# Layer 0: the prompt's value products two blocks later in the output projection

## The chip, the cores and the metric

The kernel runs on one core of one Trainium2 chip. The metric is the device time of one execution in microseconds (us). The time before the change is the median of three runs, and one execution was also taken by the hardware profiler. Engines are named as in the profile: PE (matrix multiply) with PEld (its weight loads), DVE (vector), ACT (scalar), POOL, and SP, which issues most of the transfers.

## The reference

The reference is one inference step of a two-layer decoder, for a prompt of 256 tokens and a group of 8 single-token samples that share all weights (264 columns together). Layer 0 does a root-mean-square norm, one input projection to q, k, v, bu and bv, block-sparse attention with 8 heads of 64 (on the prompt this is plain causal softmax attention in two 128-row blocks, since the block is 256 long), a gated mixer on bu and bv, and one output projection, then a feed-forward network with a causal convolution of width 3. Layer 1 has stick-breaking attention and a pooling mixer in place of the two mixers. The part of layer 0 that matters here:

```
p = softmax(q k^T / 8, causal)            # prompt, per head
a = p v                                   # "value products"
y = concat(a, b_out) @ w_out              # output projection
x = x + y
```

The samples attend to 256 cached keys and values each, plus their own.

## The kernel before

**Tiles.** Activations lie transposed: 128 features on the partitions and 264 columns (256 prompt, 8 samples) along the free side. A weight block is 128x128. Weights and operands are 32-bit; each is cut into a high and a low part (`wh`/`wl`, `catA_h`/`catA_l`), and each weight block takes three matmuls: high weight by high operand, high weight by low operand, low weight by high operand. All weight blocks of the kernel stand in one hand-written order, 1472 of them, in phases `in0`, `out0`, `ff0`, `dn0`, `in1`, and so on. `in0` has 160 blocks, so block 169 of the kernel is block 9 of `out0`.

**Weights.** `raw(ci)` loads a chunk of 8 or 16 blocks from memory (tile `raw`), issued by SP; `split(t)` cuts 8 blocks at a time, the high part on ACT and the low part on DVE (line 324).

**The order of out0.** `run(order, rhs, evac, hooks)` walks the blocks and issues their matmuls (line 228 is the one line through which all matmuls go, 231 all transposes). The output projection has 8 result tiles (m) of 8 blocks (k). For the first four m the blocks k = 4..7, which read `catB` (the gated mixer), come first: 16 blocks. Then the same four m take k = 0..3, which read `catA` (attention): 16 blocks. Then come the other four m. So the first block that reads `catA` is block 16 of `out0` (block 176 of the kernel), with `catA[:, 0]`; blocks 17, 18 and 19 read `catA[:, 1]`, `[:, 2]` and `[:, 3]`.

**Hooks.** `blk(b, f)` calls `f` once `b` blocks of the phase have been issued; that is how other work on PE is put between weight blocks. In `in0` to `out1` every PE instruction is pinned to the order in which the program issues it (`fixed[0] = True`). On ACT and DVE only some instructions are pinned (`keep_in_program_order`) or tied behind one named instruction (`behind`); the rest is put in order when the program is built, by a planner that goes by its own estimates of when inputs are ready, and among ready instructions takes the one that was issued first. On the chip each engine then runs its own list.

**The work around the change.** At hook 1 of `out0`, 20 of the samples' value reductions are issued (`sm_value`, line 606, DVE, pinned). At hook 4 come `sm_out` (transposes `po_l`, copies `part_l`, additions into `osam_l`), `v_turn` (transposes `vtp_v` of v, copies to `vt` on ACT, line 638) and `sm_cut` (high part of the samples' result on ACT, line 515; low part on DVE, line 519). At the hook of the change, `s_av(t)` is called for four pairs of heads: 4 matmuls of `pT` (softmax weights, transposed) and `vt` into the PSUM tile `pav0_t`, and then `halves`, which copies the high part (`catA_h<-pav`, ACT, line 515) and the low part (`catA_l<-pav,catA_h`, DVE, line 519). In the profile a 32-bit matmul of that kind appears twice, so the four calls of a layer are 32 rows. For t > 0 the low part is tied behind the samples' low part:

```
halves(catA[0][:, t, :SEQ], catA[1][:, t, :SEQ], pav[:, :SEQ])
if t > 0:
    behind(held_by[0], st0["cut"])
```

At hook 15 `hold(23)` and `hold(24)` tie the cuts of weight tiles 23 and 24: the DVE half behind the last low part of `s_av`, the ACT half of tile 24 behind the samples' high part. Layer 1 calls its own value products, `z_av`, at hook 11 of `out1`.

Of the kernel before, what the change touches and what calls it, by code (L numbers as in the profile page):

```python
# [215 lines left out]
def tile_decoder_step(ctx: ExitStack, tc: tile.TileContext, a):  # L216
# [828 lines left out]
    blk = lambda b, f, *x: hk.at(b / 8 - 1, f, *x)  # L1045
# [66 lines left out]
    blk(15, hold, 23)  # L1112
    blk(15, hold, 24)
    for t in range(4):
        blk(9, s_av, t)
    blk(24, lnexp)


# [189 lines left out]
    blk = lambda b, f, *x: hk.at(b / 8 - 1, f, *x)  # L1308
# [163 lines left out]
```

## Time and profile before

| | before |
|---|---|
| median of 3 runs | 587.07 us (586.77 to 587.13) |
| profiled execution | 587.01 us |
| its span | 585.1 us |
| granted PE clock | 0.998 |
| PE busy | 578.1 us, 99% |
| PEld busy | 567.1 us, 97% |
| DVE busy | 444.9 us, 76% |
| ACT busy | 342.1 us, 58% |
| POOL busy | 47.7 us, 8% |
| moved by the transfers | 128.81 MB, mean 220 GB/s |

The span is what the profile covers; the profiled execution took 1.9 us more than its span. Times in the views below count from the start of the span. A row of the timeline gives the start, the duration, the engine, the line, the operation, the tile written and the tiles read, and in brackets the idle time of the engine before it and what ended it. Matmuls overlap: each lasts about 0.28 us in the record, while a new one starts every 0.12 us, so the distance of starts is what counts.

### The profile page before, as it was taken

The page shows a single profiled execution, that of the slowest core. Times are in us where ns is not written, and L with a number is a line of the kernel's source. Part 1 is how long each engine was busy: PE and PEld are TensorE (multiplying, and loading weights), DVE is VectorE, ACT ScalarE, POOL GpSimd, SP SyncE. Part 2 cuts the span into 40 slices and gives each one's busy share as a digit, 9 for nine tenths or more (in the row PEclk, how much of TensorE's full clock was granted, in tenths as well). Part 3 has the DMA queues.
Part 4 walks back from the last instruction along what each step waited for, and adds up shares of the span by engine and source line. Part 5 has one row for each costly group of instructions (what it writes and reads, how often), then busy time and mean ns, then how long its engine had stood idle before and what let it go on. Part 6 is the DMA issues. An engine that isn't in the chain of part 4 may idle for free.

```text
span 585.1 us, 12476 instructions
## 1 busy us (share of the span) xinstructions
PE 578.1 (99%) x4928; PEld 567.1 (97%) x4928; DVE 444.9 (76%) x867; ACT 342.1 (58%) x612; POOL 47.7 (8%) x62
## 2 busy tenths in 40 slices
PE   9999999999999999999999999999999999999995
PEld 8998989999999999999999889999999999999995
DVE  6999898887777778656658879977787787865561
ACT  7848848755555656544445467667565565664431
POOL 1000205300000000001130000120000000011011
PEclk9999999999999999999999999999999999999999
DMA  8999798545454555985467779655454545454502
GB/s 328 409 371 397 228 320 308 203 159 196 165 189 171 184 178 165 346 311 194 162 249 253 289 220 286 216 205 192 170 201 160 211 156 211 155 213 153 207 1 75
DMA packets 29964, 128.81 MB, mean 220 GB/s; under 512 B 3826, under 2 KB 5842, under 8 KB 18514
## 3 DMA queue, kind: packets, MB, share of 16 engines
q1 hardware_dynamic: 29472, 127.50, 61.9%
q8 instruction: 39, 0.64, 0.4%
q10 hardware_dynamic: 434, 0.51, 0.3%
q14 instruction: 19, 0.16, 0.1%
HBM read 123.94 MB, written 4.06 MB: 219 GB/s over the span
## 4 chain that ended last, share of the span: by engine, by line
PE 97%; issue 1%; POOL 0%; POOLq 0%; DVE 0%; ACT 0%; ACTq 0%
PE mm L228 91%; PE sc L228 1%; PE pav L228 1%; PE warm L228 1%; PE pt L231 1%; PE Z L228 1%; PE S L228 1%; PE pv_l L228 0%; PE pf L228 0%; PE pm L228 0%; PE vtp_v L231 0%; POOL yo L1398 0%; PE po_l L231 0%; PE vtp_sgu L231 0%; POOLq L1447 0%
## 5 line engine op out<-in xcount | busy, mean ns | idle before, releaser
L324 ACT ACTIVATE wh<-raw 128x1024 fp32r<-128x1024 f32 x177 | 187.4, 1060 | 194.8 <-PE mm L228 182.1
L324 DVE TENSOR_TENSOR wl<-raw,wh 128x1024 fp32r<-128x1024 f32 x177 | 217.3, 1229 | 100.7 <-ACT wh L324 99.9
L228 PE MATMUL mm<-xg_f_h,wh 128*128 128x264 f32 x704 | 200.8, 285 | 0.0
L228 PE MATMUL mm<-xg_f_h,wl 128*128 128x264 f32 x704 | 200.7, 285 | 0.0
L228 PE MATMUL mm<-xg_f_l,wh 128*128 128x264 f32 x704 | 199.6, 283 | 0.0
L228 PEld LDWEIGHTS mm<-xg_f_l,wh 128*128 128x128 f32 x704 | 133.1, 189 | 0.0
L228 PEld LDWEIGHTS mm<-xg_f_h,wh 128*128 128x128 f32 x704 | 132.8, 189 | 0.0
L228 PEld LDWEIGHTS mm<-xg_f_h,wl 128*128 128x128 f32 x704 | 132.5, 188 | 0.0
L228 PE MATMUL mm<-a_h,wh 128*128 128x264 f32 x352 | 100.4, 285 | 0.0
L228 PE MATMUL mm<-a_h,wl 128*128 128x264 f32 x352 | 100.4, 285 | 0.0
L228 PE MATMUL mm<-a_l,wh 128*128 128x264 f32 x352 | 99.8, 283 | 0.0
L228 PEld LDWEIGHTS mm<-a_l,wh 128*128 128x128 f32 x352 | 66.6, 189 | 0.0
L228 PEld LDWEIGHTS mm<-a_h,wh 128*128 128x128 f32 x352 | 66.4, 189 | 0.0
L228 PEld LDWEIGHTS mm<-a_h,wl 128*128 128x128 f32 x352 | 66.3, 188 | 0.0
L228 PE MATMUL mm<-xg_h,wh 128*128 128x264 f32 x160 | 42.8, 293 | 0.0
L228 PE MATMUL mm<-xg_h,wl 128*128 128x264 f32 x160 | 41.7, 284 | 0.0
L228 PE MATMUL mm<-xg_l,wh 128*128 128x264 f32 x160 | 41.5, 284 | 0.0
L228 PE MATMUL mm<-xg_n_h,wh 128*128 128x264 f32 x128 | 37.0, 289 | 0.0
L228 PE MATMUL mm<-xg_n_h,wl 128*128 128x264 f32 x128 | 36.6, 286 | 0.0
L228 PE MATMUL mm<-xg_n_l,wh 128*128 128x264 f32 x128 | 36.4, 285 | 0.0
L228 PEld LDWEIGHTS mm<-xg_h,wh 128*128 128x128 f32 x160 | 28.9, 191 | 1.6 <-issue 1.2
L228 PEld LDWEIGHTS mm<-xg_h,wl 128*128 128x128 f32 x160 | 28.7, 189 | 0.0
(268 smaller groups left out, 864.7 us busy)
## 6 DMA issues: line engine op xcount, KB each, us to landing
raw<-in_w SPq DMA_DIRECT2D x89, 1024.0 KB, 4.8
K<-in_kt SPq DMA_DIRECT2D x32, 256.0 KB, 5.2
V<-in_vt SPq DMA_DIRECT2D x24, 256.0 KB, 6.3
pb_l<-zd_l SPq DMA_DIRECT2D x24, 256.0 KB, 5.3
V<-in_vp SPq DMA_DIRECT2D x8, 256.0 KB, 7.6
raw<-in_w SPq DMA_DIRECT2D x3, 512.0 KB
xw<-in_xw SPq DMA_DIRECT2D x3, 388.0 KB
X<-in_x SPq DMA_DIRECT2D x2, 528.0 KB
```

The source lines that it names most:

```text
L228: return self.keep(nc.tensor.matmul(*x, **k))
L231: return self.keep(nc.tensor.transpose(*x, **k))
L324: for i, j in zip((s.activation(h, src, AF.Copy), v.tensor_tensor(l, src, h.bitcast(F32), ALU.subtract)), ahead.pop(tt, ())):
```

## The change

The four calls of `s_av` are hooked at block 11 of `out0` instead of block 9: on PE, the six matmuls of blocks 169 and 170 of the kernel (`catB` by the weights of the third result tile) now stand ahead of the value products instead of behind them. Nothing is added or removed, and no other hook stands between 9 and 11.

```diff
     blk(15, hold, 23)
     blk(15, hold, 24)
     for t in range(4):
-        blk(9, s_av, t)
+        blk(11, s_av, t)
     blk(24, lnexp)
```

## The prediction

> **What bounds the kernel now.** I read the page's head and the chain that ended last first, to see which engine sets the time; then the chain in order of time, for the place of the change; then the timelines of PE, ACT and DVE there, for the waits that the move could add or remove.
>
> ```profile
> span 585.1 us, 12476 instructions
> PE 578.1 (99%) x4928; PEld 567.1 (97%) x4928; DVE 444.9 (76%) x867; ACT 342.1 (58%) x612; POOL 47.7 (8%) x62
> PE 97%; issue 1%; POOL 0%; POOLq 0%; DVE 0%; ACT 0%; ACTq 0%
> PE warm L228 <- PEq L1438: 0.8, 1, 0.8
> ```
>
> The last line is all that the view of waits has for PE: one wait, before the first instruction. Everything else is a stream of matmuls. So the time changes only if the number or the pace of PE's instructions changes, or if PE starts to wait. A move that lets PE find its inputs sooner has nothing to take away. In all, 585.1 - 578.1 = 7.0 us of the span are without PE, and they lie outside the place of the change: the 0.8 us at the start, and what follows the last matmul.
>
> In the chain in order of time (start, us, what) the value products of both layers stand so:
>
> ```profile
> 81.83 2.80 PE pav L228 x32
> ...
> 364.20 2.80 PE pav L228 x32
> ```
>
> The 32 rows take 2.80 us in layer 0 at block 9 of its phase, and 2.80 us in layer 1, where they already stand at block 11 of a phase in the same order (`catB` first, then `catA`). That is the nearest row to the changed place, and it says that the place costs PE nothing by itself.
>
> **The change part by part.** PE's timeline around the place (start, us, engine, line, operation, tiles):
>
> ```profile
> 81.55 0.28 PE L228 MATMUL mm<-catB_h,wl 128*128 128x264 f32 x1
> 81.76 2.87 PE L228 MATMUL pav<-pT,vt 128*64 128x256 f32 x32
> 84.57 0.39 PE L228 MATMUL mm<-catB_h,wh 128*128 128x264 f32 x1
> 84.79 0.28 PE L228 MATMUL mm<-catB_l,wh 128*128 128x264 f32 x1
> ...
> 85.41 0.29 PE L228 MATMUL mm<-catB_h,wh 128*128 128x264 f32 x1
> ...
> 86.14 0.29 PE L228 MATMUL mm<-catB_h,wh 128*128 128x264 f32 x1
> ...
> 87.23 0.29 PE L228 MATMUL mm<-catA_h,wh 128*128 128x264 f32 x1
> 87.36 0.28 PE L228 MATMUL mm<-catA_l,wh 128*128 128x264 f32 x1
> ...
> 88.34 0.29 PE L228 MATMUL mm<-catA_h,wh 128*128 128x264 f32 x1
> 88.47 0.28 PE L228 MATMUL mm<-catA_l,wh 128*128 128x264 f32 x1
> ```
>
> *Six matmuls pass in front.* From 85.41 to 86.14 six matmuls start in 0.73 us. That is how much later the value products come: start 82.49 instead of 81.76, end of their stretch 85.30 instead of 84.57. Behind them 15 matmuls are left until `catA` instead of 21. The same work stands between 81.55 and 87.23, so `catA` is asked for at 87.23 as before. The price is 0.
>
> *Going into and out of the value products.* From the last full matmul to the first product is 81.76 - 81.55 = 0.21 us against 0.12 at pace, and from the first matmul behind them to the second 84.79 - 84.57 = 0.22: some 0.09 and 0.10 us of changeover. Both are there once before and once after, between blocks of the same result tile either way (blocks 8 to 11 are one tile). Price 0; if the place mattered, the bound from these two rows is plus or minus 0.2 us. I take 0, since layer 1 shows the same 2.80 us at block 11.
>
> *What the products wait for.* They read `vt`, whose copies are on ACT:
>
> ```profile
> 80.08 1.09 ACT L638 ACTIVATE vt<-vtp_v 128x512 f32<-128x512 f32 x2
> 82.70 0.38 ACT L515 ACTIVATE catA_h<-pav 128x256 fp32r<-128x256 f32 x1 [1.53 <-PE pav L228]
> ...
> 84.67 0.38 ACT L515 ACTIVATE catA_h<-pav 128x256 fp32r<-128x256 f32 x1 [0.27 <-PE pav L228]
> 86.55 0.23 ACT L515 ACTIVATE catA_h<-osam_l 128x32 fp32r<-128x32 f32 x1 [1.49 <-DVE osam_l L955]
> 89.03 2.01 ACT L324 ACTIVATE wh<-raw 128x1024 fp32r<-128x1024 f32 x2 [2.26 <-DMA raw<-in_w]
> ```
>
> `vt` is done at 81.17, 0.59 us before the products start, so nothing waited for it. The move makes this slack 1.32 us. That gains nothing, because the 0.59 was already above zero.
>
> *The high parts, on ACT.* Four copies follow the products, from 82.70 to 85.05. They move by 0.73: 83.43 to 85.78. ACT then sat idle until 86.55, waiting for the samples' result on DVE, and after that until 89.03 for a weight transfer. The delay fits into the first gap with 86.55 - 85.78 = 0.77 us to spare. Price 0.
>
> *The low parts, on DVE*, are what PE's `catA` blocks need last:
>
> ```profile
> 79.11 0.41 DVE L606 CUSTOM_DVE_ANT_1 pb_l<-pb_l,V 128x256 f32<-128x256 f32 x1
> ...
> 86.03 0.18 DVE L949 TENSOR_TENSOR ob<-ob,v 128x32 f32<-128x32 f32 x1
> ...
> 86.43 0.42 DVE L519 TENSOR_TENSOR catA_l<-pav,catA_h 128x256 fp32r<-128x256 f32 x1
> 86.81 0.19 DVE L519 TENSOR_TENSOR catA_l<-osam_l,catA_h 128x32 fp32r<-128x32 f32 x1
> 86.92 1.08 DVE L519 TENSOR_TENSOR catA_l<-pav,catA_h 128x256 fp32r<-128x256 f32 x3
> 87.91 1.21 DVE L324 TENSOR_TENSOR wl<-raw,wh 128x1024 fp32r<-128x1024 f32 x1
> ```
>
> From 79.11 to 86.03 DVE goes through the 20 value reductions of the samples without a gap, and these do not depend on the products. The first low part could have run at 83.08, when its high part was done, and ran at 86.43. After the move its input is there at 83.81: still 2.62 us of cover. The fourth has its input at 85.78 and starts at about 87.6. So DVE's times stay, and with them the end of the last low part, 86.92 + 1.08 = 88.00, which PE reads at 88.47. The margin of 0.47 us that PE has there is set by DVE, not by the products, and is untouched. If DVE had been free, the price would still be zero until the high parts came later than about 87.2. The cut of the next weight tile (87.91) stands behind the last low part and stays too; so do the transfers, which are issued as buffers come free behind such cuts.
>
> *PSUM banks.* The four `pav` tiles are freed by the low parts, whose times stay; nothing that follows them sooner is asked for.
>
> Sum: 0 on PE, 0 through ACT, 0 through DVE. Against the profiled execution's own 587.01 us (span 585.1 and 1.9 around it) that is 587.0 us; the median of the three runs is 587.07, 0.01% away. 0.2% or 1.2 us is about what a measurement of this kernel can tell from no change.
>
> **The rivals.** They all come from the planner: ACT's and DVE's lists are made anew, by its own estimates, and the products come later in those too. Where PE stands is pinned, so the move itself does happen.
>
> *The samples' high part goes ahead of the four copies on ACT, and costs little.* In layer 1 it is so:
>
> ```profile
> 366.02 0.23 ACT L515 ACTIVATE catA_h<-osam_l 128x32 fp32r<-128x32 f32 x1 [1.27 <-DVE osam_l L1246]
> 366.27 1.21 ACT L515 ACTIVATE catA_h<-pav 128x256 fp32r<-128x256 f32 x4
> ...
> 366.69 1.41 DVE L519 TENSOR_TENSOR catA_l<-pav,catA_h 128x256 fp32r<-128x256 f32 x4 [0.22 <-ACT catA_h L515]
> ```
>
> With the distances of these rows, the first copy would start at 86.55 + 0.25 = 86.80 and the low parts at 86.80 + 0.42 = 87.22, first one done at about 87.64. PE wants it at 87.36, so it would wait 0.3 us, and the rest would follow at PE's pace (the fourth at 87.22 + 1.41 = 88.63, wanted by then at 88.77). That gives 587.3. For it: the 0.73 us by which the copies approach the 86.55. Against it: 0.77 us remain between them on the chip's clock. If only the last copies fall behind, nothing is lost: the third and fourth would end before 87.7.
>
> *A cut of a weight tile goes ahead of the last copies on ACT: slower.* The row at 89.03 is the cut `wh` of the next tiles, which waited 2.26 us for its transfer. The planner issues it right behind the samples' high part, to which it is tied. If in the planner's estimates the last copy is not ready at that moment and the transfer has landed, the cut goes first. On the chip the copy would then start at about 89.03 + 1.0 = 90.0, its low part at 90.4, done at 90.8, where PE wants it at 88.47: a wait of 2.4 us, 589.4. It decides from the point at which the last copy is planned later than the samples' high part. For it: that cut and the copies are neighbours in ACT's list, and the transfer is late on the chip. Against it: there are 1.5 us of idle ACT between the last copy and the samples' high part, twice the shift.
>
> [...] No row here shows a ready instruction held behind a waiting one, or passing it.
>
> *Something elsewhere in the plan falls out better: faster.* PE has no wait to lose, so more than 1.2 us would have to come out of the 7.0 us at the two ends, which this hook doesn't touch, or out of the pace. If so, some 585.5.
>
> **How the numbers follow.** No change in ACT's and DVE's order, or only a harmless one: 0.76, 587.0. Samples' part ahead of the copies: 0.10, 587.3. Cut ahead of a copy: 0.07, 589.4; another new wait of over 1.2 us somewhere down the plan: 0.03. Faster by over 1.2 us: 0.04. So within 0.2% 0.86, slower 0.10, faster 0.04. The range holds the first two cases, with the spread of the runs shown (586.77 to 587.13), the changeover's 0.2 us on both sides and the 0.3 us of the first rival above: 586.5 to 587.8. The two far cases, 0.14 together, are left out.
>
> **What would show each step right or wrong.** In the trace of the changed kernel: the products at about 82.5 us and 2.80 us long; 15 matmuls between them and the first `catA` block, which starts at about 87.2 as before; the four ACT copies 0.7 us later, from about 83.4 to 85.8, still ahead of the samples' high part at 86.5; DVE's rows from 79 to 89 us at their old times; no wait of PE but the first. The prediction is wrong if PE's pace breaks between 87 and 91 us, if ACT's list has a `wh` cut or the samples' part in front of a copy of `pav`, or if the stretch from 84.6 us on ends at another distance from the end of the span than before.

## The result and the profile after

The changed kernel takes 583.29 us in the median of 14 runs, beside 587.17 us of the kernel before in the same comparison: 0.9944 of it, with a 95% interval of 0.9926 to 0.9962. That is 3.9 us faster, where 587.0 us and no change had been forecast, and below the range of 586.5 to 587.8.

The 14 times are not spread around their median. Eight lie between 582.3 and 583.4, one at 584.4, five between 586.2 and 587.8. The profiled execution is one of the last five (586.96 us, span 585.1), so the profile after shows the cause twice, once in each direction.

First, what was forecast for the place of the change itself. PE, ACT and DVE in the profile after (start, us, engine, line, operation, tiles); everything in this execution starts 0.73 us later, so 0.73 has to be taken off each start. (The chain of this execution begins with the transfers of `xw`; PE waits 0.4 us for an operand made from them, until 8.8 us, which it did not do before.)

```profile
83.22 2.87 PE L228 MATMUL pav<-pT,vt 128*64 128x256 f32 x32
86.02 0.39 PE L228 MATMUL mm<-catB_h,wh 128*128 128x264 f32 x1
...
87.94 0.28 PE L228 MATMUL mm<-catA_h,wh 128*128 128x264 f32 x1
```

```profile
84.15 0.38 ACT L515 ACTIVATE catA_h<-pav 128x256 fp32r<-128x256 f32 x1 [2.26 <-PE pav L228]
...
87.27 0.23 ACT L515 ACTIVATE catA_h<-osam_l 128x32 fp32r<-128x32 f32 x1 [0.76 <-DVE osam_l L955]
```

```profile
87.15 0.42 DVE L519 TENSOR_TENSOR catA_l<-pav,catA_h 128x256 fp32r<-128x256 f32 x1
```

The products start at 82.49, `catA` at 87.21, the copies at 83.42, the low parts at 86.42: to a few hundredths what the sum said. The lists of ACT, DVE and POOL are the same as before, so is the order of the transfers, and PE waits nowhere but at the start. Nothing was won there.

The time comes from behind it. The chain in order of time (start, us, what), first of the kernel before, then of the changed one:

```profile
84.64 26.09 PE mm L228 x211
...
111.84 195.09 PE mm L228 x1589
...
393.13 177.03 PE mm L228 x1468
```

```profile
86.08 25.03 PE mm L228 x205
111.12 0.12 PE ns_f L228
111.24 0.85 PE mm L228 x7
112.09 0.12 PE ns_f L228
112.21 191.57 PE mm L228 x1589
...
389.84 180.23 PE mm L228 x1468
```

The first row of each is the rest of the output projection of layer 0 behind the products. The first long row is the feed-forward network of layer 0 and the start of layer 1, the second long row that of layer 1 to the end. The same 1589 matmuls take 195.09 us before and 191.57 after: 122.78 and 120.56 ns each. The 1468 of the second stretch take 177.03 and 180.23: 120.59 and 122.77. So PE shows two paces here, 1.8% apart, and in this execution the two stretches have changed roles. Before, the first was slow and the second fast. In this one it is the other way round, and the 0.73 us of the late start eats the rest. Where both are fast, the time is near 582.6.

Was something else different in the first stretch? The busy times of the engines, the granted clock and the transfers in it, in the kernel before and in the changed one (columns: stretch, its length, then PE, PEld, DVE, ACT and POOL busy with their instructions, PE clock, share of the transfer engines, GB/s):

```profile
111.84:306.93 195.09, 195.09 (x1591) 195.09 (x1591) 138.00 (x225) 107.59 (x178) 9.73 (x12) 1.00 0.58 206
```

```profile
112.21:303.78 191.57, 191.57 (x1591) 191.57 (x1591) 138.14 (x226) 107.84 (x178) 9.70 (x12) 1.00 0.59 210
```

Both have the clock at 1.00, and DVE and ACT are busy for the same time within 0.3 us. PE alone is quicker. Worked out from the start times in ns, the distances between the starts of matmuls in the feed-forward network repeat every 36 matmuls, to within 0.2 ns on average, for over 100 us, at either pace. Whatever ACT, DVE and the transfers do meanwhile leaves no mark on them.

The rest of the output projection has a pace of its own. By the start times, after the first two dozen, it runs at 122.78 ns in the kernel before and at 121.11 in the changed one. The slow pace goes on into the feed-forward network. The 121.11 becomes 120.56 within some two dozen matmuls of the first `ns_f`, a single matmul of the same shape for the norm's sum; the operands change there too, from `catA` and `catB` to those of the feed-forward network. So a pace can also change where no burst of another shape stands. Which of the two does it was not tried.

### The profile page after: what moved, and what is told of

Same layout as the page of the kernel before. It is cut to its first block, busy times and chain, and to the rows that moved or that the text cites. A ratio compares the mean times of both kernels' runs of the same rounds, so it can differ in the third digit from the quotient of the medians.

```text
span 585.1 us, 12476 instructions
## 1 busy us (share of the span) xinstructions
PE 577.7 (99%) x4928; PEld 566.7 (97%) x4928; DVE 445.1 (76%) x867; ACT 342.6 (59%) x612; POOL 47.8 (8%) x62
## 4 chain that ended last, share of the span: by engine, by line
PE 96%; issue 2%; DMA 1%; ACT 0%; POOL 0%; SPq 0%; POOLq 0%; DVE 0%; ACTq 0%
PE mm L228 90%; PE sc L228 1%; DMA xw<-in_xw 1%; PE pav L228 1%; PE pt L231 1%; PE Z L228 1%; PE S L228 1%; PE pv_l L228 0%; PE pf L228 0%; PE pm L228 0%; PE vtp_v L231 0%; POOL yo L1398 0%; SPq L402 0%; PE po_l L231 0%; PE vtp_sgu L231 0%
## 5 line engine op out<-in xcount | busy, mean ns | idle before, releaser
L228 PEld LDWEIGHTS mm<-xg_l,wh 128*128 128x128 f32 x160 | 28.8, 190 | 0.0
```

The costliest lines, as they stand in the source:

```text
L228: return self.keep(nc.tensor.matmul(*x, **k))
```

## The experiments

The theory that these were made for, called the pace theory: on a long stream of matmuls PE holds one of several fixed paces; a burst of matmuls of another shape, such as the value products, lets the pace fall anew, and it is kept until the next such burst. The rivals: the later the products, the less something is held up (slack); PE's pace is set by what ACT, DVE and the transfers do beside it (contention); the products come too late for `catA` (lateness). The last part of the theory, that a pace is kept until the next such burst, does not hold everywhere: the change from 121.11 to 120.56 above is against it.

### Other places for the products

```diff
-        blk(9, s_av, t)
+        blk(10, s_av, t)      # av10; 12 in av12, 13 in av13
```

```diff
-        blk(11, z_av, t)
+        blk(9, z_av, t)       # z9, layer 1; layer 0 stays at 9
```

> The value products of layer 0 at block 10 (before: 9, changed: 11). Pace theory: on long streams PE holds one of two paces, 120.56 or 122.78 ns per matmul, and which one is settled where it comes back from the burst of value products; it keeps it until the next burst. Then this time is one of two values, about 587 (slow pace from 85 to 320 us) or about 582.5 to 583.3 (fast), and the profile shows one pace over the whole stretch. If the weight block at which PE comes back decides (9 slow, 11 fast), the value at 10 is open. Slack theory (the later the products, the less something behind them is held up): in between, about 585. Contention theory (the pace is set by ACT, DVE and transfers beside it): no relation to the place, and the pace drifts inside the stretch.

> The value products of layer 0 at block 12. Pace theory: one of two values again, 587 or 583, by the pace from 86 to 320 us. Slack theory: as the changed kernel or faster, 583 or below, at every place from 11 on. Lateness theory (the high and low parts of the value products come too late for block 16): a wait of PE shows at block 16 and the time grows from here on.

> The value products of layer 0 at block 13, four blocks after the old place, so that PE comes back at the same place within the four-block pattern of the operand tiles as at 9. Pace theory with the place within four blocks as what decides: slow as at 9, about 587, 122.78 ns per matmul. Pace theory with another thing that decides: 583 or 587. Slack theory: 583 or below.

> Layer 0 as before (block 9); the value products of layer 1 moved from block 11 to block 9. Pace theory with the place as what decides: the second stretch (from about 367 us to the end) turns slow too, 122.78 instead of 120.56 ns over some 1700 matmuls, about +3.9 us: 591. If the place alone doesn't decide: 587. Slack theory: layer 1 had no wait, within 0.3 us of before. Contention theory: no change, 587.

The two long stretches in the chain of av10, av12, av13 and z9, in this order:

```profile
112.09 191.57 PE mm L228 x1589
...
389.38 177.03 PE mm L228 x1468
```

```profile
111.82 191.57 PE mm L228 x1589
...
389.11 177.03 PE mm L228 x1468
```

```profile
111.92 195.09 PE mm L228 x1589
...
393.21 177.03 PE mm L228 x1468
```

```profile
111.94 195.09 PE mm L228 x1589
...
393.23 177.03 PE mm L228 x1468
```

Measured: av12 583.06 us (ratio 0.9925, 0.9908 to 0.9941); av13 587.15 us, ten runs from 586.9 to 588.0 (1.0005, 0.9991 to 1.0018). Block 12 is as fast as 11, and block 13 as slow as 9. The rows are equal to 0.01 us to those of the profiles above: 191.57 or 195.09, nothing between. Slack and lateness fall, since both run one way with the place; nor does PE wait anywhere but at the start in the profile of av13. av10 has 586.11 us in the median (0.9971, 0.9946 to 0.9996, without the run at 591.8), made of four runs at 582.8 to 583.3, five at 586.0 to 588.4 and one at 591.8: here it falls now one way, now the other.

z9 tells where the theory was too simple. Block 9 is slow in layer 0; in layer 1 it stayed fast in the profile, and the time at 587.33 us (1.0011, 0.9995 to 1.0028). Two of ten runs came at 590.3 and 590.7, near what both stretches slow would take; those two have no profile. The place by itself does not decide.

### Added bursts that do nothing but interrupt the stream

```diff
+    def burst(name):                       # constants; nobody reads the result
+        fixed[0] = True
+        for t in range(NCALL):             # 4 in probe4, 1 in probe1
+            pd = at(f"pd{name}_{t}")
+            for hh in range(2):
+                o = pd[64 * hh:64 * hh + 64, :SEQ]
+                pe.matmul(o, CST[:, 0:HD], CST[:, :SEQ], start=True, stop=False)
+                pe.matmul(o[:, P:], CST[:, P:P + HD], CST[:, :P], start=False, stop=True)
...
+        for b in (PROBES0, PROBES1)[l]:
+            pk.at(b / 8 - 1, burst, f"{l}_{b}")
-        run(orders[f"ff{l}"], lambda m, k: hl(xg, k), evac)
+        run(orders[f"ff{l}"], lambda m, k: hl(xg, k), evac, pk)
+        fixed[0] = False
```

> The kernel before (products of layer 0 at block 9), with 14 added bursts of 16 matmuls of constants in the form of the value products (128x64 weights, 256 and 128 columns, results read by nobody): in ff0 behind blocks 64, 105, 146, 187, 228, 269, 310, in ff1 behind blocks 71, 112, 153, 194, 235, 276, 317, each at another place of the eight-block pattern. Their own cost is 14 x 2.8 = 39 us. Pace theory: each stretch of 41 blocks between two bursts has one pace throughout, 120.56 or 122.78 ns per matmul, and it can change at a burst and nowhere else, in ff0 (which comes in slow) as in ff1 (which comes in fast). If the block at which PE comes back decides, the same place gives the same pace in both layers. Contention theory (ACT, DVE, transfers): ff0 stays at 122.8 and ff1 at 120.6, or the pace drifts; a burst changes nothing.

> The same with bursts of 4 matmuls instead of 16 (14 x 0.7 = 10 us). Pace theory: a short burst is as good as a long one at letting the pace fall anew; a stretch behind the same place then has the same pace as with 16. Contention theory: no change of pace at a burst.

Each took one execution: 629.07 and 599.77 us, of which the bursts themselves are 39 and 11 us by their rows. The chain of probe4, the six full stretches between bursts in layer 0 and then those in layer 1 (line numbers are 3 higher in kernels with the burst; the rows of the bursts between them are left out):

```profile
131.80 15.10 PE mm L231 x123
149.71 15.11 PE mm L231 x123
167.62 15.30 PE mm L231 x123
185.72 15.09 PE mm L231 x123
203.61 15.29 PE mm L231 x123
221.71 15.28 PE mm L231 x123
...
434.08 15.29 PE mm L231 x123
452.17 15.10 PE mm L231 x123
470.07 15.11 PE mm L231 x123
487.98 15.30 PE mm L231 x123
506.09 15.09 PE mm L231 x123
523.98 15.29 PE mm L231 x123
```

The 123 matmuls take either 15.09 to 15.11 us or 15.28 to 15.30. The difference of 0.19 us is 1.5 ns for each, so the shorter ones are not at 120.56 but at a third pace of 121.1 ns (their start times give 121.06 to 121.12, after the first 12). In these rows the pace changes at a burst and holds between bursts, while ACT, DVE and the transfers go on with the work of the same layer. That speaks against contention, though not by itself: ACT and DVE have their work in another order in these two kernels than in the kernel before.

The bursts stand behind blocks whose numbers modulo 8 are 0, 1, 2, 3, 4, 5 for the first six rows and 7, 0, 1, 2, 3, 4 for the last six: 0, 1 and 3 give the middle pace in both layers, 2 and 4 the slow one in both. So with equal bursts the outcome repeated at all five places that the layers share. At each of them PE also came in at the same pace in both layers (slow at 0 and 3, middle at 1, 2 and 4), so the place and the pace ahead of the burst can't be told apart here.

With bursts of 4 matmuls (probe1) the pace also falls anew, in three values, the first two stretches of layer 0 and the fifth, then the second and the fifth of layer 1:

```profile
129.69 15.10 PE mm L231 x123
145.59 15.03 PE mm L231 x123
...
193.22 15.28 PE mm L231 x123
...
433.73 15.28 PE mm L231 x123
...
481.66 15.04 PE mm L231 x123
```

15.03 is the fast pace, 120.56. Places do not match between the layers here: behind a block divisible by 8 it is 15.10 in layer 0 and 15.28 in layer 1. The expectation that a short burst does the same as a long one at the same place missed. Of the five shared places only 2 gave one pace twice. At 0, 1 and 4 PE came in at another pace in the other layer; at 3 it came in at the middle pace both times, and left at the middle one in layer 0 and at the fast one in layer 1.

### One burst as a cure, and one as a harm

cure25 is the kernel before with one burst of 4 matmuls behind block 25 of `ff0`, harm66 the changed kernel with one burst of 16 behind block 66. In cure25 the lists of the other engines are untouched.

```diff
+PROBES0 = (25,)        # cure25, NCALL = 1;  harm66: (66,), NCALL = 4
```

> The kernel before, value products at block 9, and one added burst of 4 matmuls of constants (as in the run probe1, 0.9 us by its rows) behind block 25 of ff0; DVE, ACT, POOL and SP have the same lists as before. Pace theory: the place of the value products does not matter as such; the burst lets the pace fall anew, some 1750 matmuls before the next burst. If it comes back at 120.56 ns: -1750 x 2.22 ns + 0.9 = -3.0, 584.1; at 121.1 ns (the third pace that the bursts showed): 585.1; if it falls slow again: 588.0. Slack theory (something about the value products was late at block 9): more work on PE can only cost, 588.0.

> The changed kernel, value products at block 11, and one added burst of 16 matmuls of constants behind block 66 of ff0, place 2 of the eight-block pattern, behind which the pace was slow in both layers of the run probe4. Pace theory: from there to the next burst, some 1630 matmuls, the pace turns from 120.56 to 122.78 ns: +3.6 us beside the burst's own 2.9 us, so that the changed kernel's 583.3 becomes 589.8, with the stretch ahead of the burst still fast. Slack theory: the gain of the change stays, 583.3 + 2.9 = 586.2.

The chain of cure25 behind its burst, then that of harm66 ahead of and behind it:

```profile
115.12 190.00 PE mm L231 x1567
```

```profile
111.14 17.49 PE mm L231 x145
...
131.42 175.11 PE mm L231 x1444
```

In cure25 the products stand at block 9 and the stretch behind the burst runs at 190.00 / 1567 = 121.25 ns, the middle pace. The forecast for that was 585.1 us; five of ten runs came at 584.7 to 585.8, the profiled one among them (584.72), one at 586.35 and four at 588.1 to 589.2. The median is 586.08 us beside 587.16, but as a ratio it is 0.9994 (0.9971 to 1.0018): it helps in some executions and costs its 0.9 us or more in others. More work on PE and less time, with the products where they were: in the profiled execution that is shown, as a version it is worth nothing.

harm66 missed its forecast of 589.8 us: 586.64 us, ratio to the kernel before 0.9989 (0.9966 to 1.0011). The pace ahead of the burst is 17.49 / 145 = 120.6 ns and behind it 175.11 / 1444 = 121.3, the middle and not the slow one. With 2.9 us for the burst and 1444 x 0.6 ns = 0.9 that is 3.8 above the 582.7 of the undisturbed kernel, 586.5, close to what was measured. The same burst at the same place had given the slow pace twice in probe4, where PE came from the middle pace; here it came from the fast one. So the pace before the burst seems to count too. That was not tried by itself, and place 3 in probe1 shows that the two together do not settle it either.

### How steady the fast kernels are

after5 is the changed kernel again, av12b is av12 again, av12z12 has block 12 in both layers.

> The changed kernel again, for the spread of its times. Pace theory: the times fall into groups and not around a mean: 582.5 to 583.5 (both long stretches fast), about 586.3 (first fast, second slow), 587 (first slow, second fast), 591 (both slow), each up to 1 us more by the start. Slack theory: one group.

> Value products of layer 0 at block 12 again. Pace theory: here the first stretch comes back fast as at 11; all four times of the first call were 582.6 to 583.2, so mostly that group, median 583.1, and faster than the changed kernel wherever that falls slow in the second stretch. Slack theory: as the changed kernel.

> Block 12 in both layers. Pace theory: the first stretch fast as with block 12 alone, the second open: 583 if fast, 586.5 if slow; it is a candidate for the best version only if it leaves the slow group more rarely than block 12 with layer 1 at 11. Slack theory: as block 12 alone.

after5: six runs, 582.6 to 583.2 (median 582.71, ratio 0.9929, 0.9906 to 0.9952). av12b: eleven runs, ten from 582.3 to 582.9 and one at 586.94 (582.59; 0.9935, 0.9914 to 0.9955). av12z12: six from 582.4 to 583.5 (582.85; 0.993, 0.9907 to 0.9954). The chain of after5 has both stretches fast:

```profile
111.40 191.57 PE mm L228 x1589
...
388.69 177.03 PE mm L228 x1468
```

None of the three can be told from the others, so no version here beats the changed kernel. Runs of 586 us and more are five of 20 with block 11 and one of 15 with block 12, but all five come from the first comparison, and why a stretch fell slow so often there is open. Only one of them has a profile.

The kernel before draws too: of its 100 runs beside all these versions, eight took 583.2 to 585.8 us and four 590.7 to 591.0. What the place changes is the odds. Below 586 us were 8 of 100 runs with block 9, 4 of 10 with block 10, 15 of 20 with 11, 14 of 15 with 12 (and layer 1 as before) and none of 10 with 13.

### What the paces hang on: the rows of the operands

```diff
-TW = 272
+TW = 264               # tw264; 268 in tw268
```

```diff
-    con.tile([P, 24], F32, name="room")
+    con.tile([P, 40], F32, name="room")     # shift64; 32 in shift32
```

All four are the kernel before with block 9 and the same instructions on every engine. TW is the distance in columns between the rows of an operand tile; the tiles' own places stay. `room` is an unused pad ahead of the tiles.

> The kernel before with the rows of the operand tiles 264 columns long in memory instead of 272: the same instructions in the same order on every engine, other addresses. If the slow pace hangs on where PE's operands lie in memory, the first stretch takes another pace than 122.78 ns and its pattern of 12 matmuls another shape: 583 or another value off 587. If it hangs on the sequence of instructions alone: 122.78 ns in the first stretch, 120.56 in the second, 587.

> The kernel before with every tile behind an unused pad moved by 64 bytes per partition; same instructions, same rows of 272 columns. If only the distance of the operand's rows counts (1088 bytes; 1056 gave one pace, 121.11): as before, first stretch 122.78, second 120.56, 587. If the absolute place of operand and weights counts: another pace in one of the stretches, 583 to 591.

> The same with 32 bytes. [...] If only the distance of rows counts: 122.78 and 120.56, 587.

> The kernel before with operand rows of 268 columns (1072 bytes). If the distance of the rows is what makes the paces, this gives a pattern and a pace of its own in both stretches, as 264 did (121.11 in both, 584.4): between 582.5 and 587, and probably one pace in both stretches. If 264 was merely another draw between the old paces: one of 120.56, 121.1 and 122.78.

The chains of tw264, tw268, shift64 and shift32:

```profile
111.39 192.45 PE mm L228 x1589
...
389.64 177.81 PE mm L228 x1468
```

```profile
111.53 192.44 PE mm L228 x1589
...
389.61 177.80 PE mm L228 x1468
```

```profile
111.83 195.09 PE mm L228 x1589
```

```profile
112.22 195.09 PE mm L228 x1589
```

With rows of 264 or 268 columns both stretches run at 192.45 / 1589 = 121.11 ns and 177.81 / 1468 = 121.12. That is the mean of the middle pace at 272 too, but not the same sequence. By the start times, the distances of the middle pace at 272 repeat every 72 matmuls and lie between 115 and 124 ns (cure25). In tw264 they repeat every 36 and in tw268 every 72, and lie between 117 and 127 in both. Other phases can differ: the rest of both output projections runs at 121.11 ns in tw264 and at 120.56 in tw268.

These runs show no groups of times any more: ten runs of tw264 from 584.1 to 584.8 (median 584.45, ratio 0.9959, 0.9944 to 0.9974), four of tw268 from 583.5 to 584.6 (584.15; 0.9948, 0.9931 to 0.9964). Moving everything by 64 or 32 bytes leaves 195.09 as it was (587.17 us, 0.9995, 0.998 to 1.0009; 587.15 us, 0.9993, 0.997 to 1.0016), with three and four of ten runs at 583.8 to 585.8, as three of 19 of the kernel before in that comparison. So the set of paces hangs on the distance between the operands' rows, at least between 272 and the two others, and not on where the tiles begin. Since ACT, DVE and POOL have the same lists in all four as in the kernel before, it also speaks against contention. What PE does with it inside, no run here can show.

## Why the prediction was wrong

**Right.** That PE sets the time and had no wait to lose; that the move costs nothing at its place; the new times of the products, the copies and the low parts; that DVE's times would stay; that ACT and DVE keep their order, which leaves both planner rivals without effect. The 2.4 us of the second one were the author's estimate, and no profile here shows them: in the profile after, the cut stands on ACT behind the four copies and the samples' part (copies from 84.15 us on, that part at 87.27, the cut at 89.81), and PE has no wait there.

**The step that failed** is the one on going into and out of the value products. It priced the changeover by the 0.09 and 0.10 us at its two ends and bounded the effect of the place by plus or minus 0.2 us, taking layer 1's equal 2.80 us as the proof that the place costs nothing by itself. The products do take 2.80 us everywhere. What the place changes is the pace of the some 2000 matmuls behind them: at most 2000 x 2.2 ns = 4.4 us, some twenty times the bound. By the rows of the profiles before and after5 it is 4.3 us: 0.3 in the rest of the output projection, 3.5 in the long stretch and 0.5 behind it. How the place sets the pace stays open. The prediction names the pace as a thing that could change the time, and as a source of the faster rival, which got 0.04 and 585.5 us; both times it was set aside without a row that would have given it a price.

**The number was in the profile of before.** The two rows of the chain shown above, 195.09 us for 1589 and 177.03 us for 1468 matmuls of the same shape, differ by 1.8% at the same clock of 1.00. The prediction quoted the products' rows from that view and did not divide the rows between them. With 122.78 and 120.59 ns on the table, "the pace of the first stretch is lost or won at the burst in front of it" would have been a rival with a price of 4.4 us and a gain to some 582.6. No row of before could have told which way it would fall; a chance well above 0.04 for it, and a low end at 582, could have been had from there.

## What to carry to other kernels

Divide the long rows of the chain by their counts before pricing anything: two stretches of the same instruction at two paces are a term of the sum, even when no wait shows (here 122.78 and 120.59 ns). In this kernel, which PE bounds, an edit that only moves a burst of other-shaped matmuls was worth 3.9 us of 587.2, 0.7%, through the pace behind it, and going from block 12 to 13 cost as much (583.06 and 587.15 us). So look at the times of several runs for groups, and try neighbouring places before crediting a reason. Changing the row distance of the operand tiles took the lottery away in the 14 runs here, at 121.11 ns: between the fast and the slow draw.

## What the runs showed of the hardware that was not expected

PE held, for the same stream of 128x128 weights and 264 columns with rows 1088 bytes apart, one of three paces: 120.56, 121.1 or 122.78 ns per matmul. It kept one for up to 240 us (122.78, from 85 to 329 us of the kernel before), while DVE and ACT were busy for 138.00 and 107.59 of 195.09 us beside it, and changed it at bursts of matmuls of another shape (15.09 to 15.30 us for 123 matmuls between bursts in probe4), 4 of which (0.8 us) were enough (15.03 to 15.28 in probe1). It also changed without such a burst, from 121.11 to 120.56 at the start of the feed-forward network (after, after5). With rows 1056 or 1072 bytes apart it had 121.11 to 121.12 ns in both feed-forward stretches of the one profile taken of each. Equal bursts of 16 matmuls gave equal paces in both layers of one execution (probe4), equal bursts of 4 did not (probe1), and two executions of one program could differ (the changed kernel: 582.33 to 587.75 us in 14 runs of one comparison).
